# Key normalisation of the second token tile without TensorE transposes: key roots and token roots spread over rows by way of DRAM

## Chip, core and metric

One Trainium2 chip, one core of it. The metric is the device time of one execution in microseconds (us), here the median of three. Engines are called by their short names: PE (TensorE), DVE (VectorE), ACT (ScalarE), POOL (GpSimd), SP (SyncE, which only issues DMAs here).

## What is computed

One layer of a hybrid decoder block on x of 2048 tokens by 1024 channels, float32. Cut to the lines that matter here:

```python
h = rms_norm(x, norm_g)                       # one root per token
u = jnp.einsum('bsd,dc->bsc', h, w_in)        # all input projections
v_c, b_c, c_c, z_c, q, k, v, z_a, gate_logits = jnp.split(u, SPLIT_POINTS, axis=-1)
q = rms_norm(q.reshape(b, s, 16, 64), q_norm_g)   # one root per token and head
k = rms_norm(k.reshape(b, s, 4, 64), k_norm_g)    # 4 key heads of 64 channels
o = sliding_window_attention(q, k, v, sinks) * jax.nn.silu(z_a)
```

Around it stand a gated short convolution, two output projections, sigmoid gates, a last projection and the residual. `rms_norm` multiplies by `rsqrt(mean(x*x) + eps)`; what the change touches is how the sums of squares are formed and how their roots reach the values.

## The kernel before

**Tiles and products.** The 2048 tokens are worked on in two tiles of T = 1024 (t = 0 and 1), each in two halves of H = 512. A projection is done in units of two by two blocks with a scheme of seven products in place of eight: the products come in the order 1, 5, 6, 2, 7, 3, 4 and are named X (1, 2), V (5, 3) and Y (6, 7, 4) by the PSUM bank they go to. One product is 12 matmuls of 128x512 (four pairs of operand blocks, each as high by high, high by low, low by high part) and is one **tick**. The weights of a unit come in raw (`_raw`), DVE forms sums of them, ACT casts the high part (`_ah`, `_sh`, `_th`, `_d`), and DVE subtracts for the low part (`_al`, `_sl`, `_tl`), always for the unit that follows. Tile 1 runs its units in the order of the string `SEQ1`: ga0+ga1, k, v, q0, q1, q2, cv0, q3 and so on; attention steps are laid between them at the ticks of `AT1`, the first of them in the unit cv0.

**What sets the order.** The kernel writes its own order for every engine. `put(n, f)` files a piece of work under tick n; `run` issues one product, then the pieces filed for that tick. So each engine goes through a fixed list, and an instruction that waits holds all behind it on its engine. The short steps of a reciprocal square root (`rsqrt`, L270 to L279, on DVE) are woven one at a time between other DVE instructions. ACT evacuates PSUM, squares, and casts; POOL issues the writes to DRAM; SP issues the loads of weights and of attention operands. A DMA issued by POOL also waits for the one issued eight before it, because eight semaphores are used in turn.

**Keys of tile 1 (`fin_k`, L868 to L905).** A finished key quarter `k_t` (128 channels by 512 tokens; i picks the pair of heads, q the half of the tokens) is copied from PSUM. PE turns it by four 128x128 transposes (`turn4`, L694) into a bank `ptk`; ACT copies that out as `k_n` (L880) and squares the bank (L768); DVE sums each head's 64 squares per token (`kss`, L773). After the fourth quarter the roots are taken, and DVE multiplies the four `k_n` by them (L899), the roots lying along the partitions as the tokens do. Three, five, seven and nine ticks later `back` turns a quarter back by four transposes (`pbk`), and `k_out` (L755) splits it: ACT casts `k_h`, DVE subtracts `k_l`, and POOL writes both twice to DRAM (`kd`), from where attention loads them.

**Token roots of tile 1.** `h_stats` (during tile 0) takes the roots of tile 1's tokens two blocks of 128 at a time and copies them into small tiles `rt` (DVE, L593). `h_prep` turns them into rows: `x_roots` has four transposes of a broadcast column for each half (`ptr`, L600), and ACT copies the bank to `rb` (L602), 128 equal rows of 512 roots, with which DVE scales the channels `h` (L609).

**Queries as the pattern.** For the later heads `fin_q` already forms sums of squares another way: DVE turns `q_t` in blocks of 32 into a PSUM bank `ptq` (`vec.transpose`, STREAM_TRANSPOSE in the profile), ACT squares it, DVE sums over 32, and `squares_sum` (L781) adds the two halves of each head with four small ACT copies `q_g` and four small DVE adds `q_b`.

Of the kernel before, what the change touches and what calls it, by code (L numbers as in the profile page):

```python
# [8 lines left out]
F32 = mybir.dt.float32  # L9
# [6 lines left out]
P = 128  # L16
# [84 lines left out]
def block_kernel(  # L101
# [40 lines left out]
    def mbank(name):  # L142
        return ps_m.tile([P, HB, P], F32, tag="m", name=name)
# [10 lines left out]

    vd = dram.tile([NKV, HD, S // HD + 2, P], F32, name="vd")
    od = [dram.tile([KC, P, T], F32, name=f"od{t}") for t in range(NT)]
    ocd = [dram.tile([KC, P, T], F32, name=f"ocd{t}") for t in range(NT)]
    ycd = [dram.tile([KC, P, T], F32, name=f"ycd{t}") for t in range(NT)]
    hd = [None] + [dram.tile([KC, P, T], F32, name=f"hd{t}") for t in range(1, NT)]
# [428 lines left out]

        nc.scalar.activation(out=xt if junk is None else junk, in_=xt, func=AF.Square, accum_out=ss[:, i : i + 1])

    def x_rsqrt(t, b0, n, ss, dst):
        ms = small.tile([P, n], F32, tag="sm", name=f"ms{t}_{b0}")
        return rsqrt(ms, n, f"hr{t}_{b0}", ss, 1.0 / D, lambda r: nc.vector.tensor_copy(dst, r))  # L593

    def x_roots(t, q, rs, pt=None):

        if pt is None:
            pt = mbank(f"ptr{t}_{q}")
        for b in range(HB):
            nc.tensor.transpose(pt[:, b, :], rs[:, b : b + 1].to_broadcast([P, P]), ident)  # L600
        rb = slot([P, H], F32, f"rb{t}_{q}")
        nc.scalar.copy(rb, pt.rearrange("p b q -> p (b q)"))  # L602
        return rb
# [96 lines left out]
    class KV:  # L700
# [47 lines left out]
        def back(self, i, q):  # L748
            pt = mbank(f"pbk0_{i}_{q}")
            for b in range(HB):  # L750
                nat = self.nats[2 * q + b // 2]
                nc.tensor.transpose(pt[:, b, :], nat[:, b % 2, i * P : (i + 1) * P], ident)
            k_out(0, i, q, pt)

    def k_out(t, i, q, pt):  # L755

        nm = f"k{t}_{i}_{q}"
        hi, lo = slot([P, H], F32R, f"{nm}_h"), slot([P, H], F32R, f"{nm}_l")
        split(hi, lo, pt.rearrange("p b q -> p (b q)"))
        for e in range(2):  # L760
            for l, src in enumerate((hi, lo)):
                nc.gpsimd.dma_start(
                    kd[t][2 * i + e, :, l, hs(q)].rearrange("(o d) t -> d o t", d=HD),
                    src[HALVES[e]].bitcast(F32).unsqueeze(1).to_broadcast([HD, 2, H]))
# [101 lines left out]
        return fin  # L866

    def fin_k(t):  # L868
        ss = small.tile([P, 32], F32, tag="ss", bufs=3, name=f"kss{t}")
        nats = {}  # L870

        def fin(i, q, val):
            nm = f"k{t}_{i}_{q}"
            kt = slot([P, H], F32, f"{nm}_t")
            into(kt, val)

            def sums():
                pt = turn4(kt, f"pt{nm}")
                nat = slot([P, H], F32, f"{nm}_n")
                nc.scalar.copy(nat, pt.rearrange("p b q -> p (b q)"))  # L880
                sq = head_square(pt, nm)
                put(tick[0] + 1, lambda: reduce(nat, sq))

            def reduce(nat, sq):
                nats[i, q] = nat
                head_reduce(sq, ss, 2 * i + q)
                if len(nats) == 4:
                    put(tick[0] + 1, rms)

            put(tick[0] + 1, sums)  # L890

        def rms():
            head_rms(ss, f"k{t}", scaled)

        def scaled(r):
            for n, (i, q) in enumerate(nats):
                ns = nats[i, q].rearrange("p (h d) -> p h d", d=HD)
                o = (2 * i + q) * 8
                mul(ns, ns, r[:, o : o + 8].unsqueeze(2).to_broadcast([P, 8, HD]))  # L899
                put(tick[0] + 3 + 2 * n, lambda i=i, q=q: back(i, q))  # L900

        def back(i, q):
            k_out(t, i, q, turn4(nats[i, q], f"pbk{t}_{i}_{q}"))

        return fin  # L905

# [425 lines left out]
    def h_stats(t, n0):  # L1332

        st = x_state(t)
        xs, rt, seen_ = st["x"], {}, {}

        def ld(b):
            xs[b] = upool.tile([P, 2 * H + 2], F32, tag="u", name=f"x{t}_{b}")[:, 0:D]
            r0 = t * T + b * P
            nc.gpsimd.dma_start(xs[b], x2[r0 : r0 + P, :])  # L1340

        def square(b):
            if b % 2 == 0:
                st["ss"][b] = small.tile([P, 2], F32, tag="sx", bufs=4, name=f"ss{t}_{b}")
            x_square(xs[b], st["ss"][b - b % 2], b % 2)

        def norm(b0):
            q, i = divmod(b0, HB)
            if i == 0:
                rt[q] = small.tile([P, HB], F32, tag="sr", bufs=2, name=f"rt{t}_{q}")  # L1350
            seen_[b0] = x_rsqrt(t, b0, 2, st["ss"][b0], rt[q][:, i : i + 2])

        for b in range(NB):
            put(n0 + 2 * b, lambda b=b: ld(b))
            put(n0 + 2 * b + 3, lambda b=b: square(b))
            if b % 2:
                put(n0 + 2 * b + 4, lambda b=b: norm(b - 1))
                put(n0 + 2 * b + 6, lambda b=b: seen_[b - 1]())
        st["rt"] = rt

    def h_prep(t, n0):

        st = x_state(t)
        rb = {}

        def roots(q):
            if q == 0:
                rb["banks"] = ps_s.tile([P, 2, HB, P], F32, tag="s", name=f"ptr{t}")
            rb[q] = x_roots(t, q, st["rt"][q], rb["banks"][:, q])

        for q in range(2):
            put(n0 + H_AT[0] + q, lambda q=q: roots(q))
        for j in range(KP):
            r = {}

            def ld(q, j=j, r=r):
                for p in range(2):
                    r[p, q] = slot([P, H], F32, f"h{t}_{q}_{2 * j + p}")
                    c = 2 * j + p
                    nc.gpsimd.dma_start(  # L1380
                        r[p, q], xt2[c * P : (c + 1) * P, t * T + q * H : t * T + (q + 1) * H])

            def norm(q, j=j, r=r):
                for p in range(2):
                    x_norm(r[p, q], 2 * j + p, rb[q])
                    if (p, q) != (0, 1):
                        nc.gpsimd.dma_start(hd[t][2 * j + p, :, hs(q)], r[p, q])

            n = n0 + 1 + H_AT[j]
            for q in range(2):  # L1390
                put(n + q, lambda q=q, f=ld: f(q))
                put(n + q + 3, lambda q=q, f=norm: f(q))
            sums_of(("h", t), j, r, nc.gpsimd, n + 7)
# [119 lines left out]
    rooted = {}  # L1513

    def roots(q):
        rooted[q] = x_rsqrt(0, q * HB, HB, st["ss"][q], rtok[:, q * HB : (q + 1) * HB])

    def turned(q):
        rooted[q]()
# [204 lines left out]
```

## Time and profile before

| | |
|---|---|
| three runs | 1901.0, 1904.33 and 1905.2 us, median 1904.33 us |
| profiled execution | 1904.2 us |
| its span in the profile | 1902.5 us, so 1.7 us lie around it |
| granted TensorE clock, mean | 0.999 |
| stage of the units q1 and q2 of tile 1 | about 989 to 1028 us from the span's start |

In the timeline rows, the first number is the start in us from the span's start and the second the time from the first start to the last end of the group; then come engine, line, operation, output and inputs by the names above, shapes and count, and in brackets the idle time of that engine before the row and what ended it. Matmuls overlap, so the pace of PE is read from start to start. A row of waits gives engine, tile and line, what was waited for, then us in total, times, and the longest.

### The profile page before, as it was taken

Reading aid. Unit: us, or ns where it says so; the run is one execution under the profiler, and the core shown is the slowest. Engines: PE = TensorE matmul, PEld = TensorE weight load, DVE = VectorE, ACT = ScalarE, POOL = GpSimd, SP = SyncE. Lnnn points to the kernel's source line nnn. Section 1 sums busy time; section 2 is a strip of 40 time slices with the busy share of each in tenths; the row PEclk is TensorE's granted clock in tenths of the full one; section 3 lists DMA queues with packets and bytes.
Section 4 is the critical chain, followed back from the end, with each engine's and each line's share of the span. In section 5 each row is a group of like instructions: output and inputs, shape, how many; then the busy total and the mean of one; then the engine's idle time right before and its main releaser. Section 6 shows DMA issues by size and latency. Waiting matters only on the chain.

```text
span 1902.5 us, 27997 instructions
## 1 busy us (share of the span) xinstructions
PE 1887.3 (99%) x8670; PEld 1569.2 (82%) x8670; DVE 1540.4 (81%) x2576; ACT 988.7 (52%) x1985; POOL 721.6 (38%) x1022
## 2 busy tenths in 40 slices
PE   8999999999999999999999999999999999999999
PEld 7888888888888888778887888888888888888887
DVE  7989888789877889897569988888878789886654
ACT  7665554567665345344545645556666436444321
POOL 2363444465776111121055444645766311121000
PEclk9999999999999999999999999999999999999999
DMA  8386566689988878889367556767989869989653
GB/s 310 89 215 171 160 173 185 175 244 295 255 248 214 294 261 319 318 287 298 130 175 198 171 177 192 214 187 197 257 236 258 270 236 342 332 278 269 225 175 110
DMA packets 260548, 434.74 MB, mean 229 GB/s; under 512 B 33264, under 2 KB 124400, under 8 KB 260400
## 3 DMA queue, kind: packets, MB, share of 16 engines
q1 hardware_dynamic: 202848, 314.13, 50.7%
q0 software_dynamic: 57408, 118.80, 24.6%
q8 instruction: 69, 1.13, 0.2%
q14 instruction: 79, 0.65, 0.1%
q10 hardware_dynamic: 144, 0.03, 0.0%
HBM read 278.43 MB, written 154.40 MB: 228 GB/s over the span
## 4 chain that ended last, share of the span: by engine, by line
PE 78%; DVE 7%; issue 6%; DMA 5%; POOL 2%; ACT 1%; SPq 0%; DVEq 0%; POOLq 0%; ACTq 0%
PE Y L466 27%; PE Vcv L466 4%; PE Xcv L466 4%; PE Xga L466 2%; PE Xb L466 2%; PE Vb L466 2%; PE Vo L466 2%; PE Xo L466 2%; PE po L1084 2%; PE Vga L466 2%; PE Vyb L466 2%; PE Xgb L466 2%; PE Vgb L466 2%; PE Xyb L466 2%; PE Xz L466 2%
## 5 line engine op out<-in xcount | busy, mean ns | idle before, releaser
L1046 POOL DMA_DIRECT2D x<-fd x256 | 144.0, 612 | 76.5 <-DMA fd<-f 27.1
L1019 ACT ACTIVATE p<-s,st,rq 128x128 f32<-128x128 f32 x256 | 112.9, 451 | 3.5 <-DMA od<-o 1.6
L1067 POOL TENSOR_SCALAR_AFFINE_SELECT xh<-xh 64x512 fp32r<-64x512 f32 x64 | 67.6, 1056 | 123.7 <-DVE xl L256 87.1
L1039 POOL DMA_DIRECT2D fd<-f x64 | 39.0, 610 | 180.1 <-DVE f L256 153.8
L1100 POOL DMA_DIRECT2D od<-o x64 | 68.7, 1081 | 29.1 <-DMA od<-o 16.6
L466 PE MATMUL Xcv<-oph,wcv_ah 128*128 128x512 f32 x256 | 79.4, 391 | 0.0
L1290 POOL DMA_DIRECT2D md<-thyb x32 | 27.4, 867 | 102.4 <-DVE thyb L256 76.3
L1067 POOL TENSOR_SCALAR_AFFINE_SELECT xl<-xl 64x512 fp32r<-64x512 f32 x64 | 64.0, 999 | 4.4
L841 POOL DMA_DIRECT2D q2d<-q_h x64 | 44.3, 692 | 43.6 <-ACT q_h L836 38.7
L1067 POOL TENSOR_SCALAR_AFFINE_SELECT yp<-xl 64x512 fp32r<-64x512 f32 x64 | 59.1, 924 | 3.1
L1067 POOL TENSOR_SCALAR_AFFINE_SELECT yp<-yp 64x512 fp32r<-64x512 f32 x64 | 54.3, 848 | 4.2
L466 PEld LDWEIGHTS Xcv<-oph,wcv_ah 128*128 128x128 f32 x256 | 47.3, 188 | 9.4
L256 DVE SCALAR_TENSOR_TENSOR y<-u,cols,y 128x512 f32<-128x512 f32 x64 | 51.0, 797 | 3.6 <-ACT y L1129 2.5
L1019 ACT ACTIVATION_READ_ACCUMULATOR p<-s,st,rq 128x1 f32 x256 | 51.0, 199 | 0.0
L256 DVE TENSOR_TENSOR p<-p,st 128x512 f32<-128x512 f32 x64 | 48.7, 761 | 2.5
L841 POOL DMA_DIRECT2D q2d<-q_l x64 | 44.1, 689 | 16.6 <-DVE q_l L256 5.6
L466 PE MATMUL Xcv<-oph,wcv_al 128*128 128x512 f32 x128 | 49.8, 389 | 0.0
L348 ACT CAST wcv_sh<-wcv_raw 128x1024 fp32r<-128x1024 f32 x16 | 16.9, 1053 | 62.7 <-DVE wcv_raw L256 54.1
L256 DVE TENSOR_TENSOR opa<-ina,opa 128x512 fp32r<-128x512 f32 x56 | 36.2, 685 | 16.3 <-ACT opa L283 16.1
L994 PEld LDWEIGHTS s<-kq,q 128*128 128x128 f32 x256 | 45.9, 189 | 2.2
L256 DVE TENSOR_TENSOR opc<-inc,opc 128x512 fp32r<-128x512 f32 x56 | 36.3, 686 | 13.9 <-ACT opc L283 13.8
L256 DVE STREAM_TRANSPOSE f<-p 128x512 f32<-128x512 f32 x64 | 45.4, 709 | 2.1
(762 smaller groups left out, 6614.7 us busy)
## 6 DMA issues: line engine op xcount, KB each, us to landing
wcv_raw<-in_w_in SPq DMA_DIRECT2D x32, 512.0 KB, 4.2
q<-q2d SPq DMA_DIRECT2D x64, 256.0 KB, 5.0
v<-vd SPq DMA_DIRECT2D x128, 128.0 KB, 4.2
fd<-f POOLq DMA_DIRECT2D x64, 256.0 KB, 4.1
x<-fd POOLq DMA_DIRECT2D x256, 64.0 KB, 3.7
gd<-th SPq DMA_DIRECT2D x64, 256.0 KB, 3.3
wq_raw<-in_w_in SPq DMA_DIRECT2D x16, 512.0 KB, 4.8
q2d<-q_h POOLq DMA_DIRECT2D x64, 128.0 KB, 4.9
```

The source lines that it names most:

```text
L256: r = f(*args, **kw)
L348: return (lambda: nc.scalar.copy(hi, src), lambda: vec.tensor_tensor(out=lo, in0=src, in1=hi.bitcast(F32), op=ALU.subtract))
L466: nc.tensor.matmul(ps, lhsT=w[:, j, :], rhs=b[:, m, :], start=start and j == 0 and i == 0, stop=j == KP - 1 and i == 2, skip_group_check=n ...
L841: nc.gpsimd.dma_start(q2d[t][j][half, q * 2 * HB : (q + 1) * 2 * HB, i, e, :], src[HALVES[e]].bitcast(F32).rearrange("p (b x) -> p b x", x ...
L994: nc.tensor.matmul(sp[:, h, c, skip : 3 * HD], lhsT=q2[:, h, c, :], rhs=kq[:, 0, keys], start=False, stop=c == 1)
L1019: nc.scalar.activation(out=p[:, i, :], in_=sg[:, i, HD : 3 * HD], func=AF.Exp, bias=st[:, 1, i : i + 1], scale=rv[:, i // 2, i % 2 : i % 2 ...
L1039: nc.gpsimd.dma_start(fd, f)
L1046: nc.gpsimd.dma_start(x[QUADS[k]], src[k])
L1067: nc.gpsimd.affine_select(out=d4, in_=s4, pattern=[[0, 2], [-32 * sg, 2], [0, G], [-sg, 32]], compare_op=ALU.is_gt if prev else ALU.is_ge, ...
L1084: nc.tensor.matmul(po[:, cs], lhsT=v2[:, kind, :], rhs=xx[:, :, h * HD : (h + 1) * HD], start=h == 0 and n == 0, stop=n == 2, skip_group_c ...
L1100: put(tick[0] + ADD_WAIT, lambda: nc.gpsimd.dma_start(to, o[UH].rearrange("p c e q -> p (c e) q"), accum_op=ALU.add))
L1290: nc.gpsimd.dma_start(md[t][k, :, hs(q)], m, accum_op=ALU.add)
```

## The change

**Keys.** `fin_k` no longer turns the keys on PE. DVE turns `k_t` in blocks of 32 into the bank, ACT squares it, DVE sums over 32, and `squares_sum` adds the halves of a head, all as for the queries. The roots (`k_r`) are turned by one small DVE transpose (`k_rt`), written to DRAM by eight POOL DMAs (`rkd`), and read back by eight more as rows `k_*_r`: each root row of 512 tokens is spread over the 64 partitions of its head. Then (`scaled`) DVE multiplies the kept `k_t` by these rows, and `k_out` splits it from there: ACT casts `k_h` from the product, DVE subtracts `k_l`. The four quarters get this 10, 12, 14 and 16 ticks after the roots (`K_WAIT`), where `back` came 3 to 9 ticks after.

**Token roots.** `h_stats` writes each pair of root columns to DRAM (`rd`, four POOL DMAs of 128x2 single elements), and `h_prep` loads them as `rb` with two POOL DMAs that spread the row over 128 partitions.

In instructions: PE loses 40 transposes (ten groups of four: two `ptr`, four `ptk`, four `pbk`). ACT loses four copies `k_n` and two copies `rb`, and gains four small `k_g`. DVE gains four turns of 128x512, one of 128x32 and four small `k_b`, loses four copies `rt`; its four key multiplications and four `k_l` stay in number and move from the units v and q0 to q1 and q2. POOL gains 22 DMAs (4 `rd`, 2 `rb`, 8 `rkd`, 8 rows), and its 16 `kd` writes move behind writes of q0's and q1's queries (`q2d`). SP's list is the same.

**On PE**, in the unit k of tile 1, the end of product 7 (Y) and the begin of product 3 (Vk). Before:

```order
L466 MATMUL Y<-oph_7_3_9058,wk_th 128x512 x2
L466 MATMUL Y<-oph_7_3_9058,wk_tl 128x512
L694 MATMUL ptk_0_0_9388<-ident,k_0_0_t 128x128 x4
L466 MATMUL Vk_9325<-oph_3_0_9095,wk_th 128x512 x2
L466 MATMUL Vk_9325<-oph_3_0_9095,wk_tl 128x512
L466 MATMUL Vk_9325<-oph_3_1_9098,wk_th 128x512 x2
```

After (lines stand three or four lower in the changed file):

```order
L470 MATMUL Y<-oph_7_3_9049,wk_th 128x512 x2
L470 MATMUL Y<-oph_7_3_9049,wk_tl 128x512
L470 MATMUL Vk_9316<-oph_3_0_9086,wk_th 128x512 x2
L470 MATMUL Vk_9316<-oph_3_0_9086,wk_tl 128x512
L470 MATMUL Vk_9316<-oph_3_1_9089,wk_th 128x512 x2
L470 MATMUL Vk_9316<-oph_3_1_9089,wk_tl 128x512
```

The four transposes between the two products are gone; the same goes for the other nine groups.

**On DVE**, from the end of the unit q1 to q2's begin; `wq_2_*` are the weights of the unit q2. Before:

```order
L256 TENSOR_REDUCE qss_0_9653<-ptq_0_1_0_9956 128x16
L256 TENSOR_TENSOR wq_2_raw_9649<-wq_2_raw_9649,wq_2_raw_9651 128x512
L256 TENSOR_TENSOR wq_2_raw_9651<-wq_2_raw_9651 128x512
L256 TENSOR_TENSOR wq_2_raw_9651<-wq_2_raw_9651,wq_2_raw_9649 128x512
L256 TENSOR_TENSOR wq_2_raw_9649<-wq_2_raw_9649,wq_2_raw_9651 128x512
L256 TENSOR_SCALAR q_1_0_1_l<-q_1_0_1_t,gqk,q_1_0_1_h 128x512
L256 TENSOR_TENSOR wq_2_sl<-wq_2_raw_9651,wq_2_sh 128x1024
L790 TENSOR_TENSOR q_0_b<-qss_0_9653,q_0_g 32x32 x4
L270 TENSOR_SCALAR q_0_ms<-q_0_b 128x32
L256 TENSOR_SCALAR q_1_1_0_l<-q_1_1_0_t,gqk,q_1_1_0_h 128x512
L271 TENSOR_SCALAR q_0_t<-q_0_ms 128x32
L256 TENSOR_TENSOR wq_2_tl<-wq_2_raw_9649,wq_2_th 128x1024
```

After:

```order
L260 TENSOR_SCALAR q_1_1_1_l<-q_1_1_1_t,gqk,q_1_1_1_h 128x512
L260 TENSOR_TENSOR k_0_1_t<-k_0_1_t,k_0_1_r 128x512
L260 TENSOR_TENSOR k_0_1_l<-k_0_1_t,k_0_1_h 128x512
L260 TENSOR_REDUCE qss_0_9643<-ptq_0_1_0_9921 128x16
L260 TENSOR_TENSOR wq_2_raw_9639<-wq_2_raw_9639,wq_2_raw_9641 128x512
L260 TENSOR_TENSOR wq_2_raw_9641<-wq_2_raw_9641 128x512
L260 TENSOR_TENSOR wq_2_raw_9641<-wq_2_raw_9641,wq_2_raw_9639 128x512
L260 TENSOR_TENSOR wq_2_raw_9639<-wq_2_raw_9639,wq_2_raw_9641 128x512
L260 TENSOR_SCALAR q_1_0_1_l<-q_1_0_1_t,gqk,q_1_0_1_h 128x512
L260 TENSOR_TENSOR wq_2_sl<-wq_2_raw_9641,wq_2_sh 128x1024
```

and behind the four small adds `q_0_b`:

```order
L274 TENSOR_SCALAR q_0_ms<-q_0_b 128x32
L260 TENSOR_SCALAR q_1_1_0_l<-q_1_1_0_t,gqk,q_1_1_0_h 128x512
L275 TENSOR_SCALAR q_0_t<-q_0_ms 128x32
L260 TENSOR_TENSOR k_1_0_t<-k_1_0_t,k_1_0_r 128x512
L277 TENSOR_SCALAR q_0_r<-q_0_t 128x32
L260 TENSOR_TENSOR k_1_0_l<-k_1_0_t,k_1_0_h 128x512
L281 TENSOR_TENSOR q_0_t<-q_0_r 128x32
L260 TENSOR_TENSOR wq_2_tl<-wq_2_raw_9639,wq_2_th 128x1024
```

The multiplication and the low part of the quarter k_0_1 now stand ahead of the weight sums that make `wq_2_sl`, and those of k_1_0 ahead of `wq_2_tl`. In the same way those of k_0_0 stand ahead of q1's addition `Vq_1<-s5q_1,Y` and those of k_1_1 right behind it. Before, each `k_l` stood alone, from the end of v to the begin of q1.

**On ACT**, the same stretch. Before:

```order
L836 ACTIVATE q_1_1_1_h<-q_1_1_1_t,gqk 128x512
L568 COPY q_1_0_1_t<-Vq_1_9892 128x512
L836 ACTIVATE q_1_0_1_h<-q_1_0_1_t,gqk 128x512
L348 COPY wq_2_sh<-wq_2_raw_9651 128x1024
L788 COPY q_0_g<-qss_0_9653 32x32 x4
L568 COPY q_1_1_0_t<-Y 128x512
L836 ACTIVATE q_1_1_0_h<-q_1_1_0_t,gqk 128x512
L348 COPY wq_2_th<-wq_2_raw_9649 128x1024
L489 COPY Y<-Xq_2_10065 128x512
```

After:

```order
L839 ACTIVATE q_1_1_1_h<-q_1_1_1_t,gqk 128x512
L287 COPY k_0_1_h<-k_0_1_t 128x512
L572 COPY q_1_0_1_t<-Vq_1_9848 128x512
L839 ACTIVATE q_1_0_1_h<-q_1_0_1_t,gqk 128x512
L352 COPY wq_2_sh<-wq_2_raw_9641 128x1024
L791 COPY q_0_g<-qss_0_9643 32x32 x4
L572 COPY q_1_1_0_t<-Y 128x512
L839 ACTIVATE q_1_1_0_h<-q_1_1_0_t,gqk 128x512
L352 COPY wq_2_th<-wq_2_raw_9639 128x1024
L287 COPY k_1_0_h<-k_1_0_t 128x512
L493 COPY Y<-Xq_2_10050 128x512
```

The casts k_0_1_h and k_1_0_h have moved in; the second stands directly ahead of the copy of the bank Xq_2 into Y, on which q2's third product adds.

```diff
--- before.py
+++ after.py
@@ -69,6 +69,8 @@
     19, 15, 29, 29, 28, 29]
 OP_S = [12, 15, 16, 19, 21, 16, 23, 24, 16, 17, 21, 23, 27, 22, 24, 24]
 OP_K = [11, 13, 18, 21, 8, 8, 24, 34, 15, 29, 29, 31, 40, 36]
+K_LOAD = 2
+K_WAIT = 10
 SEQ0 = (
     "q0 q1 q2 q3 cv0 cv1 cv2 cv3 b0 cv4 cv5 b1 b2 cv6 cv7 b3 gb1 ga0 gb2 ga1 gb0 ga2 ga3 gb3 z0 "
     "z1 z2 z3 za0 za1 za2+za3 ya0+ya1 ya2+ya3 yb0+yb1 yb2+yb3")
@@ -154,6 +156,8 @@
 
     vd = dram.tile([NKV, HD, S // HD + 2, P], F32, name="vd")
     od = [dram.tile([KC, P, T], F32, name=f"od{t}") for t in range(NT)]
+    rd = [None] + [dram.tile([T], F32, name=f"rd{t}") for t in range(1, NT)]
+    rkd = [None] + [dram.tile([NKV, 2 * NB, HD], F32, name=f"rkd{t}") for t in range(1, NT)]
     ocd = [dram.tile([KC, P, T], F32, name=f"ocd{t}") for t in range(NT)]
     ycd = [dram.tile([KC, P, T], F32, name=f"ycd{t}") for t in range(NT)]
     hd = [None] + [dram.tile([KC, P, T], F32, name=f"hd{t}") for t in range(1, NT)]
@@ -588,14 +592,13 @@
 
         nc.scalar.activation(out=xt if junk is None else junk, in_=xt, func=AF.Square, accum_out=ss[:, i : i + 1])
 
-    def x_rsqrt(t, b0, n, ss, dst):
+    def x_rsqrt(t, b0, n, ss, then):
         ms = small.tile([P, n], F32, tag="sm", name=f"ms{t}_{b0}")
-        return rsqrt(ms, n, f"hr{t}_{b0}", ss, 1.0 / D, lambda r: nc.vector.tensor_copy(dst, r))
-
-    def x_roots(t, q, rs, pt=None):
-
-        if pt is None:
-            pt = mbank(f"ptr{t}_{q}")
+        return rsqrt(ms, n, f"hr{t}_{b0}", ss, 1.0 / D, then)
+
+    def x_roots(t, q, rs):
+
+        pt = mbank(f"ptr{t}_{q}")
         for b in range(HB):
             nc.tensor.transpose(pt[:, b, :], rs[:, b : b + 1].to_broadcast([P, P]), ident)
         rb = slot([P, H], F32, f"rb{t}_{q}")
@@ -750,13 +753,13 @@
             for b in range(HB):
                 nat = self.nats[2 * q + b // 2]
                 nc.tensor.transpose(pt[:, b, :], nat[:, b % 2, i * P : (i + 1) * P], ident)
-            k_out(0, i, q, pt)
-
-    def k_out(t, i, q, pt):
+            k_out(0, i, q, pt.rearrange("p b q -> p (b q)"))
+
+    def k_out(t, i, q, src):
 
         nm = f"k{t}_{i}_{q}"
         hi, lo = slot([P, H], F32R, f"{nm}_h"), slot([P, H], F32R, f"{nm}_l")
-        split(hi, lo, pt.rearrange("p b q -> p (b q)"))
+        split(hi, lo, src)
         for e in range(2):
             for l, src in enumerate((hi, lo)):
                 nc.gpsimd.dma_start(
@@ -866,8 +869,8 @@
         return fin
 
     def fin_k(t):
-        ss = small.tile([P, 32], F32, tag="ss", bufs=3, name=f"kss{t}")
-        nats = {}
+        ss = small.tile([P, 64], F32, tag="ss4", bufs=2, name=f"kss{t}")
+        kts = {}
 
         def fin(i, q, val):
             nm = f"k{t}_{i}_{q}"
@@ -875,32 +878,52 @@
             into(kt, val)
 
             def sums():
-                pt = turn4(kt, f"pt{nm}")
-                nat = slot([P, H], F32, f"{nm}_n")
-                nc.scalar.copy(nat, pt.rearrange("p b q -> p (b q)"))
+                pt = mbank(f"pt{nm}")
+                vec.transpose(out=pt.rearrange("p b q -> p (b q)"), in_=kt)
                 sq = head_square(pt, nm)
-                put(tick[0] + 1, lambda: reduce(nat, sq))
-
-            def reduce(nat, sq):
-                nats[i, q] = nat
-                head_reduce(sq, ss, 2 * i + q)
-                if len(nats) == 4:
+                put(tick[0] + 1, lambda: reduce(sq))
+
+            def reduce(sq):
+                kts[i, q] = kt
+                n = 2 * i + q
+                vec.tensor_reduce(
+                    out=ss[:, n * 16 : (n + 1) * 16], in_=sq.rearrange("p (h d) -> p h d", d=32),
+                    axis=AX.X, op=ALU.add)
+                if len(kts) == 4:
                     put(tick[0] + 1, rms)
 
             put(tick[0] + 1, sums)
 
         def rms():
-            head_rms(ss, f"k{t}", scaled)
-
-        def scaled(r):
-            for n, (i, q) in enumerate(nats):
-                ns = nats[i, q].rearrange("p (h d) -> p h d", d=HD)
-                o = (2 * i + q) * 8
-                mul(ns, ns, r[:, o : o + 8].unsqueeze(2).to_broadcast([P, 8, HD]))
-                put(tick[0] + 3 + 2 * n, lambda i=i, q=q: back(i, q))
-
-        def back(i, q):
-            k_out(t, i, q, turn4(nats[i, q], f"pbk{t}_{i}_{q}"))
+            both, adds = squares_sum(ss, f"k{t}")
+            vec.chain(*adds)
+            head_rms(both, f"k{t}", kept)
+
+        def kept(r):
+
+            rt = small.tile([P, 32], F32, tag="sm", name=f"k{t}_rt")
+            vec.transpose(out=rt, in_=r)
+            for a in range(4):
+                e, s = divmod(a, 2)
+                for i in range(2):
+                    to = rkd[t][2 * i + e, :, s * 32 : (s + 1) * 32]
+                    nc.gpsimd.dma_start(to, rt[32 * a + 16 * i : 32 * a + 16 * i + 16])
+            for n, (i, q) in enumerate(kts):
+                put(tick[0] + K_LOAD + n, lambda i=i, q=q: load(i, q))
+                put(tick[0] + K_WAIT + 2 * n, lambda i=i, q=q: scaled(i, q))
+
+        rows = {}
+
+        def load(i, q):
+            rb = rows[i, q] = slot([P, H], F32, f"k{t}_{i}_{q}_r")
+            for e in range(2):
+                src = rkd[t][2 * i + e, q * NB : (q + 1) * NB].rearrange("n x -> (n x)")
+                nc.gpsimd.dma_start(rb[HALVES[e]], src.unsqueeze(0).to_broadcast([HD, H]))
+
+        def scaled(i, q):
+            kt = kts[i, q]
+            mul(kt, kt, rows[i, q])
+            k_out(t, i, q, kt)
 
         return fin
 
@@ -1332,7 +1355,7 @@
     def h_stats(t, n0):
 
         st = x_state(t)
-        xs, rt, seen_ = st["x"], {}, {}
+        xs, seen_ = st["x"], {}
 
         def ld(b):
             xs[b] = upool.tile([P, 2 * H + 2], F32, tag="u", name=f"x{t}_{b}")[:, 0:D]
@@ -1345,10 +1368,10 @@
             x_square(xs[b], st["ss"][b - b % 2], b % 2)
 
         def norm(b0):
-            q, i = divmod(b0, HB)
-            if i == 0:
-                rt[q] = small.tile([P, HB], F32, tag="sr", bufs=2, name=f"rt{t}_{q}")
-            seen_[b0] = x_rsqrt(t, b0, 2, st["ss"][b0], rt[q][:, i : i + 2])
+            def kept(r):
+                nc.gpsimd.dma_start(rd[t][b0 * P : (b0 + 2) * P].rearrange("(b p) -> p b", p=P), r)
+
+            seen_[b0] = x_rsqrt(t, b0, 2, st["ss"][b0], kept)
 
         for b in range(NB):
             put(n0 + 2 * b, lambda b=b: ld(b))
@@ -1356,7 +1379,6 @@
             if b % 2:
                 put(n0 + 2 * b + 4, lambda b=b: norm(b - 1))
                 put(n0 + 2 * b + 6, lambda b=b: seen_[b - 1]())
-        st["rt"] = rt
 
     def h_prep(t, n0):
 
@@ -1364,9 +1386,8 @@
         rb = {}
 
         def roots(q):
-            if q == 0:
-                rb["banks"] = ps_s.tile([P, 2, HB, P], F32, tag="s", name=f"ptr{t}")
-            rb[q] = x_roots(t, q, st["rt"][q], rb["banks"][:, q])
+            rb[q] = slot([P, H], F32, f"rb{t}_{q}")
+            nc.gpsimd.dma_start(rb[q], rd[t][hs(q)].unsqueeze(0).to_broadcast([P, H]))
 
         for q in range(2):
             put(n0 + H_AT[0] + q, lambda q=q: roots(q))
@@ -1513,7 +1534,8 @@
     rooted = {}
 
     def roots(q):
-        rooted[q] = x_rsqrt(0, q * HB, HB, st["ss"][q], rtok[:, q * HB : (q + 1) * HB])
+        to = rtok[:, q * HB : (q + 1) * HB]
+        rooted[q] = x_rsqrt(0, q * HB, HB, st["ss"][q], lambda r: nc.vector.tensor_copy(to, r))
 
     def turned(q):
         rooted[q]()
```

## The prediction

> **What bounds the kernel now.** I read the page's busy shares first, then the chain of work that ended last, then what PE waits for, and last the timelines of the two stretches that the change touches.
>
> ```profile
> span 1902.5 us, 27997 instructions
> PE 1887.3 (99%) x8670; PEld 1569.2 (82%) x8670; DVE 1540.4 (81%) x2576; ACT 988.7 (52%) x1985; POOL 721.6 (38%) x1022
> PE 78%; DVE 7%; issue 6%; DMA 5%; POOL 2%; ACT 1%; SPq 0%; DVEq 0%; POOLq 0%; ACTq 0%
> ```
>
> ```profile
> PE ptr L600 <- DVE rtok L593: 4.4, 1, 4.4
> PE Vcv L466 <- DVE wcv_sl L256: 0.5, 1, 0.5
> PE Vq L466 <- DVE wq_sl L256: 0.3, 1, 0.3
> ```
>
> PE is busy 1887.3 of 1902.5 us: it is the bound, and whatever PE no longer does comes off the time where PE sets the pace. Its few waits matter as warnings: DVE's low part of weight sums (`wq_sl`, `wcv_sl`) already arrives 0.3 and 0.5 us late in the units q2 and cv0, so there DVE is as late as it may be. The share of 81% for DVE does not say this; the rows of the stage do.
>
> **What PE saves.** The tile view counts the transposes of tile 1, the timeline shows their price.
>
> ```profile
> L694 PE MATMUL ptk<-ident,k_t x16: 270/272/273, 939.9 to 949.8; 128*128 128x128 f32 x16
> L694 PE MATMUL pbk<-ident,k_n x16: 270/272/273, 970.5 to 989.0; 128*128 128x128 f32 x16
> ```
>
> ```profile
> 621.87 0.60 PE L600 MATMUL ptr<-ident,rt 128*128 128x128 f32 x4
> 622.23 0.71 PE L466 MATMUL Y<-oph,wz_sh 128*128 128x512 f32 x2
> ...
> 939.90 0.60 PE L694 MATMUL ptk<-ident,k_t 128*128 128x128 f32 x4
> 940.26 0.70 PE L466 MATMUL Vk<-oph,wk_th 128*128 128x512 f32 x2
> ...
> 943.09 0.60 PE L694 MATMUL ptk<-ident,k_t 128*128 128x128 f32 x4
> ...
> 991.88 0.62 PE L466 MATMUL Vq<-oph,wq_sh 128*128 128x512 f32 x2
> ...
> 994.60 0.62 PE L466 MATMUL Y<-oph,wq_sh 128*128 128x512 f32 x2
> ```
>
> From the first of four transposes to the next matmul pass 940.26 - 939.90 = 0.36 us (0.36 at 621.87 too). The product behind them takes 943.09 - 940.26 = 2.83 us; one with no transposes ahead takes 994.60 - 991.88 = 2.72. So a group costs 0.36 + 0.11 = 0.47, say 0.48 with rounding. There are ten groups (16 + 16 transposes in the two rows make eight, `ptr` two): **PE saves 10 x 0.48 = 4.8 us**.
>
> By the rows' 272 ns for one, 40 would save 10.9 us; but the starts show four passing in 0.36 us, so the sum goes by starts. The Trainium skill (TensorE: Matmul & The Clock Gate, Part 4: PE-mode transpose) also gives about 275 ns for one transpose in a kernel, 11.0 us for 40 by an estimate; the trace agrees with it as a duration (272 ns), not as a price.
>
> **What DVE, ACT and POOL take on, and what hides it.** In the units k and v of tile 1 DVE gets four turns in blocks of 32 and loses the four multiplications `k_n`.
>
> ```profile
> 955.67 0.70 DVE L256 TENSOR_TENSOR Vv<-s5v,Y 128x512 f32<-128x512 f32 x1 [3.64 <-PE Y L466]
> 963.09 2.48 DVE L256 TENSOR_TENSOR k_n<-k_n,k_r 128x512 f32<-128x512 f32 x4
> 993.40 1.31 DVE L256 STREAM_TRANSPOSE ptq<-q_t 128x512 f32<-128x512 f32 x2
> ```
>
> Four turns at 1.31/2 = 0.66 make 2.6 us, and DVE waits 3.64 us for PE's Y in one row there, so they are hidden; without that cover they would cost 2.6. The small `k_b` and `k_t` steps (bounds: nothing, and one turn of 0.66) stand where the 2.48 us of `k_n` leave. ACT loses six copies and is idle half the time: nothing.
>
> The token roots go through DRAM with much room.
>
> ```profile
> 625.56 1.08 POOL L1100 DMA_DIRECT2D od<-o  x1 [10.63 <-PE Y L466]
> 635.15 1.41 DVE L256 SCALAR_TENSOR_TENSOR h<-h,cols,rb 128x512 f32<-128x512 f32 x2
> ```
>
> POOL stands idle 10.63 us where the two loads `rb` are issued, and DVE first uses `rb` at 635.15, 13 us behind the first `ptr`. The four `rd` writes lie about 150 us earlier, among POOL's attention work; at the 1.08 us of the nearest write with many pieces they take 4.3 us in all, in four places. I take nothing for them; at worst each delays an attention step by its 1.08.
>
> The key roots need eight small writes, then eight row loads, at some 0.6 us of POOL each, and a landing time of one write and one load; they have ten ticks, 27 us, from about 963 on. The nearest landing time is that of `kd` in the list of DMA issues:
>
> ```profile
> kd<-k_h POOLq DMA_DIRECT2D x8, 256.0 KB, 5.7
> ```
>
> 16 x 0.6 + 2 x 5.7 = 21 us puts the last row at about 984 when all is in series, and at most some four us later behind twelve `vd` writes of v; the first use is at 992. I take no cost, with 5 us as the other end.
>
> **What moves into q1 and q2 is the term that decides.** DVE's multiplication there is followed by a cast on ACT that waits for it and by `k_l` on DVE that waits for the cast; nothing stands between, so DVE idles during the cast. The same hand-over exists for the queries:
>
> ```profile
> 991.05 0.57 ACT L283 CAST k_h<-pbk 128x512 fp32r<-128x512 f32 x1
> ...
> 1004.79 0.72 ACT L836 ACTIVATE q_h<-q_t,gqk 128x512 fp32r<-128x512 f32 x1 [1.17 <-DVE q_t L256]
> 1013.22 0.58 ACT L489 COPY Y<-Xq 128x512 f32<-128x512 f32 x1
> ```
>
> ```profile
> 997.59 0.70 DVE L256 TENSOR_TENSOR Vq<-s5q,Y 128x512 f32<-128x512 f32 x1 [2.13 <-PE Y L466]
> ...
> 1001.61 0.75 DVE L256 SCALAR_TENSOR_TENSOR q_l<-q_t,gqk,q_h 128x512 fp32r<-128x512 f32 x1 [1.01 <-ACT q_h L836]
> ...
> 1004.08 0.68 DVE L256 TENSOR_TENSOR q_t<-Y,s5q 128x512 f32<-128x512 f32 x1
> 1005.55 0.75 DVE L256 SCALAR_TENSOR_TENSOR q_l<-q_t,gqk,q_h 128x512 fp32r<-128x512 f32 x1 [0.79 <-ACT q_h L836]
> ...
> 1010.26 1.22 DVE L256 TENSOR_TENSOR wq_sl<-wq_raw,wq_sh 128x1024 fp32r<-128x1024 f32 x1
> ...
> 1013.08 0.17 DVE L271 TENSOR_SCALAR q_t<-q_ms 128x32 int32<-128x32 int32 x1
> ...
> 1018.39 0.68 DVE L256 TENSOR_TENSOR Vq<-s5q,Y 128x512 f32<-128x512 f32 x1
> ```
>
> ```profile
> 1011.53 0.50 PE L466 MATMUL Vq<-oph,wq_sl 128*128 128x512 f32 x1
> 1013.93 0.64 PE L466 MATMUL Y<-oph,wq_sh 128*128 128x512 f32 x2
> 1019.42 0.61 PE L466 MATMUL Y<-oph,wq_th 128*128 128x512 f32 x2
> ```
>
> From `q_t` at 1004.08 to its `q_l` at 1005.55 pass 1.47 us with a cast of 0.72; with the 0.57 of `k_h` that is 1.32, and `k_l` takes a quarter of 2.48: each quarter holds DVE for 1.32 + 0.62 = **1.94 us**. In DVE's order they fall thus:
> - k_0_0 stands ahead of `Vq` at 997.59, which waited 2.13 us for PE: absorbed.
> - k_1_1 stands behind that addition. The `q_l` at 1001.61 waited 1.01 for ACT and takes up 0.9 of it (ACT's square of the tile turned behind k_1_1 now comes late as well): 1.0 us left.
> - k_0_1 stands ahead of the weight sums of q2, with no wait behind it: 1.94.
>
> So `wq_sl` ends 1.0 + 1.94 = 2.9 us later, and PE, which had just waited for it at 1011.53, waits **2.9 us** more. Next, `k_1_0_h` stands on ACT directly ahead of the copy of X into Y. DVE reaches the multiplication behind the row of 1013.08, now at 1013.25 + 2.9 = 1016.15, ends it at 1016.8, the cast ends at 1017.35, and the copy (0.58) at 1017.95, against 1013.80 before. PE comes to its Y product at 1013.93 + 2.9 = 1016.85: another **1.1 us**. Last, DVE is now 2.9 + 1.94 = 4.85 late at the `Vq` of 1018.39, which ended 0.4 ahead of PE's use at 1019.42; PE is 4.0 late, so **0.4 us** more. The bounds of these three: nothing, if DVE finds room (next part), and 9.0, if nothing is absorbed.
>
> **Sum**, against the profiled execution of 1904.2 us: -4.8 + 2.9 + 1.1 + 0.4 = -0.4, so 1903.8. The median of the runs is 1904.33, 0.1 above; the runs lie 4 us apart, and about 0.2% (3.8 us) is what a measurement of this kernel can tell from no change.
>
> **A rule against the change.** A wait may also cost clock. After the one long wait of before, 4.4 us, the windows show (span, then busy time of PE, PEld, DVE, ACT, POOL, granted clock, DMA share, GB/s):
>
> ```profile
> 27.00:30.00 3.00, 2.60 (x9) 2.24 (x10) 2.96 (x7) 2.29 (x5) 0.00 (x0) 0.53 1.03 410
> 30.00:35.00 5.00, 5.00 (x22) 4.12 (x21) 5.00 (x9) 5.00 (x10) 0.00 (x0) 0.94 1.01 397
> ```
>
> The clock fell to 0.53 and cost 3 x 0.47 + 5 x 0.06 = 1.7 us. The new waits are shorter (2.0 for `wq_sh`, 0.9 for `wq_sl`, 1.1 for Y, with matmuls between), so I leave 1.7 us out; with it the time is 1905.5. The Trainium skill (TensorE: Matmul & The Clock Gate, Why this matters for your kernels) warns of idle gaps over about 3 us, since one idle window throttles; by that rule 2.9 us in one piece would be on the edge. The trace agrees for 4.4 us; no row shows 2 to 3 us.
>
> **Rivals.**
> - *The stage has room, and the saving stays.* The windows of the stage:
>
> ```profile
> 990.00:1020.00 30.00, 30.00 (x132) 24.36 (x131) 24.78 (x49) 17.39 (x30) 21.79 (x33) 1.00 0.94 253
> 1020.00:1050.00 30.00, 29.49 (x132) 23.73 (x131) 28.25 (x57) 17.00 (x31) 10.97 (x16) 1.00 0.55 139
> ```
>
>   DVE is busy 24.8 of 30 us from 990 on, so 5.2 are free; four multiplications and three more `k_l` are 7 x 0.62 = 4.3. By the budget they fit: 1904.2 - 4.8 = 1899.4, to 1900.4 if a third of the loss of `wq_sl` remains. Against it: most of the free time lies ahead of 1002, and the hand-overs are idle time, not work.
> - *The backlog is not absorbed and is carried on: slower.* From 1020 on DVE is busy 28.25 of 30 us and cannot catch up. If k_0_0 and k_1_1 also cost their full 1.94 (their casts behind other work on ACT), the loss is 4 x 1.94 + 1.1 + 0.4 = 9.3: 1908.7. It decides where DVE arrives at the `Vq` of 997.59 later than PE's Y.
> - *Rows or writes come late.* DMA is 0.94 busy from 990 to 1020, and 16 `kd` writes move into it. A row that lands after 992 holds DVE, and slots wait for `q2d` writes; each us is a us. 5 us on the forecast: 1908.8.
> - *The transposes were free.* If PE was held by others wherever they stood, nothing is saved and the stage still loses 4.4: 1908.6. Against it: PE's starts follow without a gap.
>
> **Chances.** Forecast 0.45 (1903.8, by itself 1902 to 1906), with the clock 0.05; the stage has room 0.23; transposes at 272 ns each 0.01 (1904.2 - 10.9 + 4.4 = 1897.7); backlog carried 0.18; late rows 0.05; free transposes 0.03. Faster by over 0.2%: 0.24; within: 0.50; slower: 0.26. The range reaches to both main rivals, 1899.2 to 1909.0.
>
> **What would show it.** In the changed profile: no `ptk` and no `pbk` at the end of the units k to q0, and products of 2.72 there (gain right); PE waiting about 3 us on `wq_sh` or `wq_sl` of q2 and about 1 on ACT's Y (loss right); DVE waiting 0.6 for `k_h` behind each multiplication. PE without waits in q2 would mean the first rival; `k_t` waiting for a DMA, the third; PE waits of over 6 us from q1 to cv0, the second.

## The result and the profile after

The changed kernel takes 1917.99 us (median of six runs, 1913.98 to 1918.84) against 1904.02 us before: ratio 1.0073, 95% interval 1.0063 to 1.0084. It is **slower by 14 us**; the forecast was no change, 1903.8, and the range ended at 1909.0. The profiled execution has a span of 1917.1 us.

The page of the changed kernel, in the lines that answer to the first ones of before:

```profile
span 1917.1 us, 27947 instructions
PE 1889.6 (99%) x8630; PEld 1568.9 (82%) x8630; DVE 1540.7 (80%) x2581; ACT 987.7 (52%) x1983; POOL 733.9 (38%) x1044
PE 76%; DMA 8%; issue 7%; DVE 5%; POOL 3%; ACT 1%; SPq 0%; POOLq 0%; DVEq 0%; ACTq 0%
```

The 40 transposes are gone, yet PE is busy longer (1889.6 against 1887.3), and DMA's share of the chain went from 5% to 8% (a hint only: it is 7% in two runs below that lose no time). To find the place, compare when the same product begins in both. In the tile views (last columns: first and last start) of before:

```profile
L466 PE MATMUL Xga<-oph,wga_ah x128: 387/389/423, 418.2 to 1358.9; 128*128 128x512 f32 x128
L466 PE MATMUL Xz<-oph,wz_ah x128: 387/389/477, 575.3 to 1508.7; 128*128 128x512 f32 x128
```

and of after:

```profile
L470 PE MATMUL Xga<-oph,wga_ah x128: 387/389/423, 419.0 to 1373.9; 128*128 128x512 f32 x128
L470 PE MATMUL Xz<-oph,wz_ah x128: 387/389/423, 589.9 to 1523.6; 128*128 128x512 f32 x128
```

The lag is 0.8 us at 418 and 14.6 at 575: **13.8 us are lost between them**, in tile 0's attention stage, where the change adds only the four writes `rd` of the token roots. The other half of the change, by timeline rows of before and after:

```profile
926.30 0.62 PE L466 MATMUL Xk<-oph,wk_ah 128*128 128x512 f32 x2
1027.68 0.62 PE L466 MATMUL Xcv<-oph,wcv_ah 128*128 128x512 f32 x2
```

```profile
939.44 0.62 PE L470 MATMUL Xk<-oph,wk_ah 128*128 128x512 f32 x2
1041.85 0.62 PE L470 MATMUL Xcv<-oph,wcv_ah 128*128 128x512 f32 x2
```

From the first product of k to the first of cv0 pass 101.4 us before and 102.4 after: the keys' part is nearly even, as forecast.

What happened at 440 to 500 us stands in the windows (PE, PEld, DVE, ACT, POOL, clock, DMA share, GB/s), of before and of after:

```profile
440.00:460.00 20.00, 19.87 (x98) 16.64 (x97) 18.05 (x50) 13.20 (x36) 11.00 (x16) 1.00 0.98 292
460.00:480.00 20.00, 18.90 (x91) 15.66 (x90) 17.25 (x40) 13.56 (x31) 14.00 (x20) 1.00 0.93 270
480.00:500.00 20.00, 20.00 (x101) 16.94 (x100) 14.90 (x27) 14.28 (x36) 14.64 (x20) 1.00 0.99 269
```

```profile
440.00:460.00 20.00, 18.11 (x88) 15.00 (x87) 14.64 (x45) 10.85 (x25) 8.22 (x13) 1.00 0.98 206
460.00:480.00 20.00, 16.75 (x71) 13.19 (x70) 13.82 (x30) 10.96 (x27) 13.50 (x17) 0.91 1.15 227
480.00:500.00 20.00, 15.81 (x63) 12.42 (x62) 11.71 (x23) 11.39 (x30) 9.94 (x14) 0.84 1.03 212
```

The DMA engines were full before (0.93 to 0.99) and are full after, but move 206 to 227 GB/s in place of 269 to 292. The rate in slices of 2 us from 420 to 500 us, before and after:

```profile
GB/s 209 228 311 341 346 404 415 325 242 248 214 136 237 350 403 419 307 236 280 339 263 246 269 152 342 348 275 282 287 238 175 210 276 302 356 321 312 204 254 281
```

```profile
GB/s 270 224 261 329 319 392 387 347 99 93 128 240 286 280 358 401 97 91 99 84 348 282 357 277 302 274 148 52 70 158 372 177 98 69 66 283 296 291 258 205
```

After, it falls four times, to between 52 and 148, at 436, 452, 472 and 484 us. The rows of line 1372 in the changed kernel name what began shortly before each: the writes `rd`, issued at 430.0, 447.6, 468.5 and 478.7 us.

```profile
L1372 POOL DMA_DIRECT2D rd<-hr_r x4: 718/742/755, 430.0 to 478.7; - x4
DMA to landing us min/median/max: 9.5/11.0/11.1
```

Each of the four writes carries 1 KB and takes 11.0 us to land (median), while POOL spends only 0.74 us to issue it. The bytes are not the load, and neither is the time of their own packets: in the trace's list of DMA packets of 420 to 500 us the four writes are 64 packets of 64 bytes, 22 ns each (median). The other packets grow: the longest of 4 KB takes 6.4 us, before 1.4.

So the other transfers of the stage land late. DMA issues of 420 to 480 us, with the median us to landing in the last column, before and after:

```profile
gd<-th SPq DMA_DIRECT2D x10, 256.0 KB, 4.7
wgb_raw<-in_w_in SPq DMA_DIRECT2D x2, 512.0 KB, 10.3
```

```profile
gd<-th SPq DMA_DIRECT2D x10, 256.0 KB, 8.3
wgb_raw<-in_w_in SPq DMA_DIRECT2D x2, 512.0 KB, 14.3
```

PE's waits of 400 to 500 us after (before: one row, `s <- DMA lows<-kd`, 1.1 us):

```profile
PE Y L470 <- DVE th L260: 3.1, 1, 3.1
PE po L1107 <- POOL yp L1090: 2.4, 2, 1.9
PE s L1013 <- DMA lows<-kd: 1.9, 1, 1.9
PE po L1107 <- POOL xl L1090: 1.2, 2, 0.8
PE po L1107 <- POOL xh L1090: 0.5, 1, 0.5
PE Y L470 <- DVE Vga L260: 0.3, 1, 0.3
```

They add up to 9.4 us, 8.3 more than before. The clock of 0.91 and 0.84 in the windows of 460 and 480 us costs, by an estimate that takes the whole window as run at it, 20 x 0.09 + 20 x 0.16 = 5.0 more. Together 13.3 of the 13.8. Most of the rows name DVE and POOL as the ones waited for, but these were late themselves. Ahead of the wait of 3.1 us, the chain of work that ended last shows a DMA (start, us):

```profile
479.85 10.99 DMA gd<-th
490.92 0.69 ACT th L1182
495.15 5.06 PE Y L470 x11
```

ACT's `th` had waited 6.5 us for this write `gd<-th`, which frees its tile. Ahead of `yp`, POOL's write `od` at 460.17 us had waited 6.0 us for the landing of another `od`; by the turn of eight semaphores it also had to wait for the second `rd`, which landed at 458.75. How much of the loss goes by way of POOL's queue and how much by the loads and writes of the others was not separated.

### The profile page after: what moved, and what is told of

Same layout as the page of the kernel before. It is cut to its first block, busy times and chain, and to the rows that moved or that the text cites. A ratio compares the mean times of both kernels' runs of the same rounds, so it can differ in the third digit from the quotient of the medians.

```text
span 1917.1 us, 27947 instructions
## 1 busy us (share of the span) xinstructions
PE 1889.6 (99%) x8630; PEld 1568.9 (82%) x8630; DVE 1540.7 (80%) x2581; ACT 987.7 (52%) x1983; POOL 733.9 (38%) x1044
## 4 chain that ended last, share of the span: by engine, by line
PE 76%; DMA 8%; issue 7%; DVE 5%; POOL 3%; ACT 1%; SPq 0%; POOLq 0%; DVEq 0%; ACTq 0%
PE Y L470 26%; PE Vcv L470 5%; PE Xcv L470 4%; PE Xo L470 2%; PE Vo L470 2%; PE Vyb L470 2%; PE po L1107 2%; PE Vb L470 2%; PE Xgb L470 2%; PE Xb L470 2%; PE Xz L470 2%; PE Xyb L470 2%; PE Vz L470 2%; PE Xga L470 2%; PE Vgb L470 2%
```

## The experiments

**Theory A**: the four `rd` writes, 256 single elements each, hold up the DMA queues, and what waits behind them stops PE. **Rivals**: the keys' part carries the loss (K); POOL waits for DVE's roots at the head of its queue, whatever is written (B); the rows that are loaded come late (C).

### The two parts apart

`keys_alone` is the kernel before with the edits to `fin_k` and `k_out` only; `roots_alone` with those to `h_stats` and `h_prep` only.

> Only the keys' part of the change; the token roots are turned by TensorE as before. Theory A (the token roots' four DRAM writes of 256 single elements each fill the DMA queues and cost 13.8 us at 430 to 500 us; the keys' part saves 3.8 us and loses some 4.8 in q1 and q2): 1905 us, within 0.2% of before, and no slow stretch at 430 to 500. Rival K (the keys' part carries the loss): 1916 to 1918 us.

> Only the token roots' part of the change; the keys are turned by TensorE as before. Theory A: 1904 + 13.8 - 1.0 = 1916.8 us, the loss at 430 to 500 us. Rival K: 1903 us, the two groups of transposes saved and nothing lost.

Measured: keys_alone 1904.06 us, ratio 1.0006 (0.9998 to 1.0015); roots_alone 1920.66 us, ratio 1.0092 (1.0078 to 1.0106), both against 1903.41. Rival K is out: the token roots carry the whole loss. It is 17 us here and 13.8 in the whole change; the stage's delays are not the same to the microsecond in two programs.

### What of the roots' part it is

```diff
 # roots_runs: h_stats, in place of one write of r for each pair of blocks
+                nc.vector.tensor_copy(rt[q][:, i : i + 2], r)
+                if i:
+                    nc.vector.transpose(out=rtt, in_=rt[q])
+                    for a in range(4):
+                        to = rd[t][hs(q)].rearrange("(b a x) -> a b x", a=4, x=32)
+                        nc.gpsimd.dma_start(to[a], rtt[32 * a : 32 * a + HB])
 # writes_dead: x_rsqrt of the kernel before, for tile 1
+                nc.gpsimd.dma_start(rd[t][b0 * P : (b0 + 2) * P].rearrange("(b p) -> p b", p=P), r)
```

> As the token roots' part alone, but the roots of each half are first turned by VectorE in blocks of 32, so that they go to DRAM in eight writes of four runs of 128 bytes each, from the same places in the GpSimd queue, behind the same roots. Theory A (the single elements are the cost): 1903 us, no loss at 430 to 500. Rival B (GpSimd waits for VectorE's roots at the head of its queue, whatever the writes look like): 1915 us or more.

> The kernel before with the four writes of 256 single elements added; nobody reads them, TensorE still turns the roots. Theory A: 1904 + 13.8 = 1918 us. Rival C (the loss comes from the rows being loaded and waited for, not from the writes): 1904 us.

Measured: roots_runs 1903.18 us, ratio 0.9999 (0.999 to 1.0008); writes_dead 1919.7 us, ratio 1.0094 (1.0079 to 1.011). The writes alone, read by nobody, cost all of it, so rival C is out. Turned into runs of 128 bytes, written in the same stretch and waiting for the same roots, they cost nothing that can be measured; this speaks against rival B, though the eight writes stand at two of the four places. (dead_spaced below has all four places and the same roots to wait for, and costs nothing either: rival B is out.) The landing lines of the writes in writes_dead and in roots_runs:

```profile
DMA to landing us min/median/max: 9.3/10.6/11.3
```

```profile
DMA to landing us min/median/max: 3.1/4.3/5.4
```

### Count of pieces, size of pieces, or their addresses

Both kernels are writes_dead with another shape of the same four writes: pieces of 64 bytes side by side, or pieces of 4 bytes that lie 512 bytes apart.

```diff
 # dead_64B
+                to = rd[t][16 * b0 * P : 16 * (b0 + 2) * P].rearrange("(b p x) -> p b x", p=P, x=16)
+                nc.gpsimd.dma_start(to, ident[:, 0:32].rearrange("p (b x) -> p b x", x=16))
 # dead_spaced, rd being T rows of 128 elements
+                to = rd[t][b0 * P : (b0 + 2) * P, 0:1].rearrange("(b p) x -> p b x", p=P)
+                nc.gpsimd.dma_start(to, r.unsqueeze(2))
```

> The kernel before with four writes that nobody reads, at the places of the four root writes, again 256 pieces each, but a piece is 64 bytes (constants) in place of 4: 16 KB each. If the count of pieces is the cost: 1919 us as with 4 bytes, landing 10 us. If the small size of a piece is the cost: 1904 to 1908, landing 5 to 7 us, as the writes of 256 pieces of 512 bytes that the kernel has anyway land.

> The kernel before with the four dead writes of 256 pieces of 4 bytes, but each piece goes to a block of 512 bytes of its own in DRAM in place of 128 pieces in one block. If pieces that fall in one block hold each other up: 1904 to 1906 us, landing 5 to 7 us. If each small piece is dear by itself: 1919 us, landing 10 us.

Measured: dead_64B 1902.88 us, ratio 1.0003 (0.9994 to 1.0012); dead_spaced 1902.34 us, ratio 0.9999 (0.9989 to 1.0008). I had thought a small piece dear by itself. It is not: 256 pieces of 4 bytes cost nothing when each has a block of 512 bytes of its own. The landing lines of dead_64B and dead_spaced:

```profile
DMA to landing us min/median/max: 2.4/4.2/6.5
```

```profile
DMA to landing us min/median/max: 2.2/4.8/6.8
```

So **it is the neighbourhood**: pieces of 4 bytes, from 128 partitions, are dear when they go to consecutive addresses. The packets of writes_dead and dead_spaced are alike in count, size and own time (64 of 64 bytes, 22 and 25 ns); but the longest 4 KB packet of 420 to 500 us takes 7.4 us in writes_dead and 1.9 in dead_spaced. The Trainium skill (DMA: Bandwidth & Descriptors, Specifications) says that transfers below 512 bytes are done as read-modify-write. By that alone the spaced pieces would be as dear as the others, and they are not. If read-modify-writes of one block had to follow each other, it would fit (to 512 bytes there are 128 pieces in writes_dead, eight in dead_64B, one in dead_spaced), but this is not shown: no run here tells what happens inside. From which distance on pieces of 4 bytes are free was not tried either.

### Does it matter where the writes fall

> The kernel before with four dead writes of 256 pieces of 4 bytes (constants) issued in tile 1's unit k, about 940 to 950 us, where GpSimd is idle and the DMA engines are half idle. If the cost is that they hold up loads that the busy stage waits for: 1904 to 1906 us, though landing still takes some 10 us. If a dead write costs its 3.5 us anywhere: 1918 us.

```diff
 # dead_quiet: fin_k, sums        (source: a constant)
+                nc.gpsimd.dma_start(
+                    rd[t][b0 * P : (b0 + 2) * P].rearrange("(b p) -> p b", p=P), ident[:, b0 : b0 + 2])
 # dead_quiet_2: fin_k, reduce    (source: the tile k_n of that quarter)
+                nc.gpsimd.dma_start(
+                    rd[t][b0 * P : (b0 + 2) * P].rearrange("(b p) -> p b", p=P), nat[:, 0:2])
```

Measured: 1908.51 us, ratio 1.0031 (1.0019 to 1.0043). This run missed its place: a constant has nothing to wait for, and POOL, idle, issued all four at 893 to 895 us, at the end of a busy stage. The load `inh<-hd` then landed in 18.7 us, before in 11.8; ACT waited 7.6 us for it, PE for two operands, and the clock fell, as the timeline and a window of this run show:

```profile
910.48 0.70 PE L467 MATMUL Y<-oph,wga_th 128*128 128x512 f32 x2 [1.97 <-ACT oph L284]
912.90 0.79 PE L467 MATMUL Y<-oph,wga_tl 128*128 128x512 f32 x1 [1.72 <-DVE wga_tl L257]
```

```profile
910.00:920.00 10.00, 7.80 (x21) 5.92 (x22) 9.88 (x15) 7.19 (x12) 0.00 (x0) 0.66 0.65 212
```

> As dead_quiet, but the four dead writes take their 4-byte pieces from tiles that are written at about 942 to 950 us, so that they can't be issued earlier than the stretch where the DMA engines are busy a sixth of the time. If the cost is only what waits behind them in the busy DMA queues: within 2 us of before, though each takes 10 us or more to land. If each costs PE its time anywhere: 1908 us or more, as in dead_quiet.

Measured: 1903.74 us, ratio 0.9999 (0.9989 to 1.0008). Its writes began at 940.9 to 950.8 us and were as slow as ever:

```profile
DMA to landing us min/median/max: 9.7/10.3/13.4
```

In this stretch no row of PE, ACT or DVE waits for a transfer, and 10 us of slow landing cost nothing. The price is that of what stands behind the writes.

### The keys: what takes the saving back, and a version that keeps it

`keys_split` takes the hand-over apart: multiplication, cast, and `k_l` with its writes in three successive ticks. `keys_early` is that with `K_WAIT = 6` in place of 10. `change_with_runs` is the whole change with the writes of roots_runs, `best` is that with the keys of keys_early.

```diff
         def scaled(i, q):
-            kt = kts[i, q]
-            mul(kt, kt, rows[i, q])
-            k_out(t, i, q, kt)
+            mul(kts[i, q], kts[i, q], rows[i, q])
+            put(tick[0] + 1, lambda: high(i, q))     # k_h <- k_t on ACT
...
+            put(tick[0] + 1, lambda: low(i, q, hi))  # k_l on DVE, the four kd writes
```

> The keys' part alone, with the hand-over taken apart: the multiplication in one tick, the cast k_h a tick later, k_l and the writes a tick after that. If VectorE's idle time in the hand-over (2.5 us over four quarters) and the cast ahead of the copy into Y carry the loss in q1 and q2: PE's waits there fall from 3.6 us to 1 to 2, 1901.5 to 1902.5 us. If it is VectorE's added work alone: 1904 us as before, waits unchanged.

> The keys' part alone with the hand-over taken apart over three ticks and all four quarters four ticks earlier (6 ticks after the roots in place of 10), so that they end in q0 and q1 and leave q2's weight sums alone. If the loss of q1 and q2 is the work in front of wq_sl and of the copy into Y: PE's waits in q2 go back to 0.5 us and the 3.8 us saved remain, 1899 to 1900.5 us. If the rows land too late for that, VectorE waits for them: 1903 or more.

> The whole change, but with the token roots written in runs of 128 bytes after one VectorE turn of each half. If the single-element writes are the one cause of the loss and the parts add: 1903 + 0.6 (keys) - 0.2 (roots in runs) = 1903.5 us, no change against before. If something else of the two parts together costs time: over 1907.

> keys_early and the roots in runs together. If the parts add: 1898.5 to 1900.5 us, faster than before by some 0.2%. If not: 1903.

| kernel | us | ratio (95%) |
|---|---|---|
| keys_split | 1903.31 | 1.0002 (0.9993 to 1.0011) |
| keys_early | 1899.71 | 0.9984 (0.9975 to 0.9993) |
| change_with_runs | 1904.73 | 1.0008 (0.9999 to 1.0017) |
| best | 1900.09 | 0.9985 (0.9977 to 0.9994) |

PE's waits in q1, q2 and the begin of cv0, in the timelines of keys_alone, keys_split and keys_early:

```profile
1000.00 3.01 PE L469 MATMUL Y<-oph,wq_d 128*128 128x512 f32 x12 [0.43 <-DVE q_t L259]
1007.26 0.73 PE L469 MATMUL Vq<-oph,wq_sh 128*128 128x512 f32 x2 [1.52 <-ACT wq_sh L351]
1008.70 0.50 PE L469 MATMUL Vq<-oph,wq_sl 128*128 128x512 f32 x1 [0.71 <-DVE wq_sl L259]
1012.26 0.73 PE L469 MATMUL Y<-oph,wq_sh 128*128 128x512 f32 x2 [0.99 <-ACT Y L492]
1030.31 0.50 PE L469 MATMUL Vcv<-oph,wcv_sl 128*128 128x512 f32 x1 [0.53 <-DVE wcv_sl L259]
```

```profile
1007.28 0.73 PE L469 MATMUL Vq<-oph,wq_sh 128*128 128x512 f32 x2 [0.32 <-ACT wq_sh L351]
1008.72 0.50 PE L469 MATMUL Vq<-oph,wq_sl 128*128 128x512 f32 x1 [0.71 <-DVE wq_sl L259]
1011.53 0.73 PE L469 MATMUL Y<-oph,wq_sh 128*128 128x512 f32 x2 [0.26 <-ACT Y L492]
1018.34 0.73 PE L469 MATMUL Y<-oph,wq_th 128*128 128x512 f32 x2 [1.06 <-DVE Vq L259]
1030.74 0.50 PE L469 MATMUL Vcv<-oph,wcv_sl 128*128 128x512 f32 x1 [0.54 <-DVE wcv_sl L259]
```

```profile
1006.77 0.51 PE L469 MATMUL Vq<-oph,wq_sl 128*128 128x512 f32 x1 [0.69 <-DVE wq_sl L259]
1026.78 0.50 PE L469 MATMUL Vcv<-oph,wcv_sl 128*128 128x512 f32 x1 [0.52 <-DVE wcv_sl L259]
```

Taking the hand-over apart shortens the waits for `wq_sh` and for ACT's Y, as expected, but DVE's work is still in front, and `Vq` is then late (1.06 us): 4.2 us of waits become 2.9, and the time does not tell the two kernels apart. Four ticks earlier only 1.2 us of waits are left; before, it was 0.8 (0.3 for `wq_sl`, 0.5 for `wcv_sl`, as the prediction's list of waits shows). Of the 3.8 us that eight groups are worth, 3.4 should then stay; by the ratio 3.0 us do (1.3 to 4.8). Whether the four ticks would do it without taking the hand-over apart was not tried. The parts add up: the whole change with runs is keys_alone's even result, and `best` equals keys_early within the measurement. That the two groups `ptr` (1 us) are saved as well can't be told from these runs.

## Why the prediction was wrong, point by point

- **What PE saves**: right. Eight groups of the keys are gone, and the products that followed them take 2.72 us; keys_early, with 0.4 us more of waits than before, keeps 3.0 (1.3 to 4.8) of the 3.8 us.
- **k and v: turns in blocks of 32 hidden; rows in time**: right. The eight `rkd` writes and the row loads land in 1.5 to 5.2 us, and no multiplication waits for them (one `q_l` on DVE waits 0.8 us for such a row).
- **The hand-over in q1 and q2**: right in mechanism and nearly in size. The forecast was 4.4 us of new waits: 2.9 for `wq_sh` and `wq_sl`, 1.1 for ACT's Y, 0.4 for `Vq`. In the changed kernel they are these:

```profile
1015.40 3.01 PE L470 MATMUL Y<-oph,wq_d 128*128 128x512 f32 x12 [0.43 <-DVE q_t L260]
1022.66 0.73 PE L470 MATMUL Vq<-oph,wq_sh 128*128 128x512 f32 x2 [1.52 <-ACT wq_sh L352]
1024.11 0.50 PE L470 MATMUL Vq<-oph,wq_sl 128*128 128x512 f32 x1 [0.72 <-DVE wq_sl L260]
1027.66 0.73 PE L470 MATMUL Y<-oph,wq_sh 128*128 128x512 f32 x2 [0.95 <-ACT Y L493]
```

  2.2 for the weights (0.3 of it was there before), 0.95 for Y, none for `Vq`, and 0.43 in a place that I had not named. By the starts of Xk and Xcv above, 3.8 us saved became 1.0 lost, so the stage lost 4.8: these waits, and slower products around them (2.80 to 2.87 us in place of 2.72). The granted clock stayed at 1.00. The upper bound of 9.0 given for the three terms is added wrongly: the same parts make 9.3, as under the rival of the backlog; nothing else hangs on it.
- **The token roots: here it failed.** The step was "The four `rd` writes lie about 150 us earlier ... I take nothing for them; at worst each delays an attention step by its 1.08." It was wrong in two ways. I priced the writes by the time POOL needs to issue them (0.74 us in the end), not by the time until they land. And I took the nearest row by the number of pieces: `od` has 256 pieces of 512 bytes each, `rd` 256 pieces of 4 bytes at consecutive addresses, which are another thing. No row of the prediction is from 430 to 480 us; the DMA share there, 0.93 to 0.99, warns that work waits for transfers and that landing times decide. It does not say by itself that a write is dear: dead_64B adds 16 times the bytes in the same stretch and loses nothing. In place of 0 the term was 13.8 us.
- **Rivals**: the case "rows or writes come late" was thought for the keys, at 990 us, at 5 us and a chance of 0.05. What happened is its twin at 440 us, where transfers came late; that small writes can make them so was in no rival.

## What to carry to other kernels

Price a DMA by its landing time in the stage where it is issued and by what queues behind it, not by the issuing engine's row or its bytes: look at the DMA share and GB/s of that stage first. Don't write a column of partitions as single elements to consecutive addresses; turn it first, and write runs, or write where nobody waits. Where two engines hand a value back and forth, put the work where nobody needs the engine in between: the steps in successive ticks took 1.3 us of waits away and no time that could be measured, and with four ticks earlier the kernel was 3 us faster than before.

## What the runs showed of the hardware that was not expected

- Four writes of 256 pieces of 4 bytes, 1 KB each: 10.6 us to land and 16 us of time with consecutive addresses; 4.8 us and no time with addresses 512 bytes apart; 64-byte pieces side by side 4.2 us. Full DMA engines moved 214 GB/s with the first (480 to 500 us), 269 before.
- The granted clock fell to 0.91 and 0.84 in two windows of 20 us whose longest waits were 1.9 and 3.1 us, and not in q2, where waits of 1.52, 0.72 and 0.95 us came within 6 us.
